# Mixture of experts: TensorE's order fixed by edges, weights asked for as far ahead as buffers allow, four single PSUM banks

## The chip, the core and the metric

The kernel is one program on one core of a Trainium2 chip. The metric is the device time of one execution in microseconds (us); lower is better. TensorE is called PE here, its loading of the stationary operand PEld, VectorE is DVE, ScalarE is ACT, GpSimd is POOL, and SP is the engine whose queue issues every load of weights.

## The reference

Two blocks of a small hybrid model run one after the other on 512 tokens of width 1024. The change lies in the last part of the first block, a mixture of experts:

```python
# 32 experts of width 512; each token has 2 experts with weights (gates)
def run(args):                       # a block of rows with one expert e
    tok_b, e = args
    xb = v_pad[tok_b]                # gather
    hu = xb @ w_e_in[e]              # (1024 x 1024)
    a, u = jnp.split(hu, 2, axis=-1)
    return (jax.nn.silu(a) * u) @ w_e_out[e]     # (512 x 1024)
ys = ys * rows_w[:, None]
out = jnp.zeros((T + 1, D)).at[rows_tok].add(ys) # scatter
```

All weights are float32. The experts hold 32 x (4 MB + 2 MB) = 192 MB of them, and each is read once.

## The kernel before

A list scheduler reorders the instructions that the code traces: it puts on each engine's queue what it holds to be ready first, so the order in the code is not the order on the engine. An engine then runs its queue strictly in that order.

**The experts stage** (`experts`) works on 16 pairs of experts, each expert with up to 64 rows. A pair's first product takes 8 slabs of `w_expert_in` for each of the two experts, its second product 4 slabs of `w_expert_out` for each. A slab is 128 x 1024 float32, 512 KB; a pair takes 24 slabs. `side_by_side` (line 1126) issues, for one slab of each expert and one half `c` of the columns, one product for expert 0 in the left 64 columns of the array and one for expert 1 in the right 64. Each such product is two MATMUL records in the profile, so a pair has 64 records with `sx` (first product) and 32 with `hT` (second).

**Around the products.** Every second pair, `gather` (line 1098) builds the rows `sx` of the next four experts by one-hot products: 8 units of 8 matmuls, each unit into one PSUM bank (`s`), which ACT or DVE copies away (line 1099). In the other pairs, `scatter` (line 1111) adds the results `y` of two pairs to `h`: 8 units of 4 matmuls, each unit into one `s` bank, which DVE adds (line 1113). After a pair's first product, ACT applies silu (line 1189), DVE multiplies (line 1190), and four PE transposes (line 1148) give `hT`, which the second product needs. In the code, three units stand ahead of the transposes and five behind. The second product of a pair stands two slab rows into the first product of the next pair.

**Buffers.** Slabs go through a ring of 22 buffers (10 + 12), with 7 more at the start (`raw_tile`). SP issues one load per slab and waits for a buffer whose products are done. PSUM has `self.banks(3, 0, 2)`: three tiles `g` of two banks for the products, and two single banks `s` for units and transposes.

**Overflow.** After pair 8, a branch (`overflow`, lines 1223 and 1232) reads a count; the loop behind it is for experts with more than 64 rows, and it is not entered in the profiled execution. It takes four buffers of the ring.

Of the kernel before, what the change touches and what calls it, by code (L numbers as in the profile page):

```python
# [3 lines left out]

# [14 lines left out]
P = 128  # L19
D = 1024  # L20
KT = D // P
NM = 16
S = 512
NT = S // P
# [6 lines left out]
NE = 32  # L31
ROWS = 64
OVER = 8
CAP = ROWS
HL = 4
EARLY = 7
RAWS = 10
RAWS2 = 12
# [78 lines left out]
class Builder:  # L117
# [781 lines left out]
        pool = self.early if early else self.mr if m < RAWS else self.mr2  # L899
        return self.t(pool, (P, D), tag="raw")  # L900

    def raw_slab(self, src):
        raw = self.raw_tile()
        self.nc.sync.dma_start(raw, src)
        return raw

    def proj_residual(self, first):

# [174 lines left out]
    def gather(self, xp, G):  # L1083

        nc, C = self.nc, self.C
        og = xp.tile([P, NT, 256], F32R, tag="og", name=self.nm("og"), bufs=1)
        for i in range(NT):
            a, b = (self.keyg[:, G, n * NT + i : n * NT + i + 1] for n in range(2))
            o = og[:, i]
            nc.vector.tensor_scalar(o, C["iota"][:, :256], a, None, OP.is_equal)  # L1090
            nc.vector.scalar_tensor_tensor(o, C["iota"][:, :256], b, o.bitcast(F32), OP.is_equal, OP.add)
        sx = xp.tile([P, KT, 256], F32, tag="sx", name=self.nm("sx"), bufs=1)
        yield sx
        for k in range(KT):
            p = self.p1()[:, :256]
            for hl in range(2):
                for i in range(NT):
                    nc.tensor.matmul(p, self.v[hl][:, i, k * P : (k + 1) * P], og[:, i], start=hl == 0 and i == 0, stop=hl == 1 and i == NT - 1)
            (nc.vector.tensor_copy if k % 2 else nc.scalar.copy)(sx[:, k], p)
            yield  # L1100

    def scatter(self, ys, last=False):

        nc, h2 = self.nc, self.h2
        more = [x[:, c] for x in (self.pg(), self.pg()) for c in range(2)] if last else []
        for n in range(2 * NT):
            i, c = n % NT, n // NT
            p = more.pop(0) if last and 2 <= n < 6 else self.p1()
            for a, (os_, y) in enumerate(ys):
                for hl in range(2):  # L1110
                    nc.tensor.matmul(p, os_[:, i * P : (i + 1) * P], y[c][:, hl], start=a == 0 and hl == 0, stop=a == len(ys) - 1 and hl == 1)
            x = h2[:, i, c * 512 : (c + 1) * 512]
            nc.vector.tensor_tensor(x, x, p, OP.add)
            yield

    def experts(self, es, early, routing):


        nc, io, C = self.nc, self.io, self.C
        xp = self.pool("ex", 2, es, side="right")  # L1120
        self.nraw = 0

        def side_by_side(out, x, ws, c, k, n):
            for e in range(2):
                o = slice(64 * e, 64 * e + 64)
                nc.tensor.matmul(out[o], x[:, o], ws[e][:, c * 512 : (c + 1) * 512], start=k == 0, stop=k == n - 1)  # L1126

        def slabs(src, pr, k):
            return [self.raw_slab(io[src][2 * pr + e][k * P : (k + 1) * P]) for e in range(2)]

        def one_hot(pr):

            os_ = yp.tile([P, S], F32R, tag="os", name=self.nm("os"), bufs=3)
            sid = C["slotid"][:, pr : pr + 1]
            kr, gr = self.rows
            t = yp.tile([P, S], F32, tag="ost", name=self.nm("ost"), bufs=1)
            nc.gpsimd.tensor_scalar(os_, kr[:, 0], sid, None, OP.is_equal)
            nc.gpsimd.tensor_scalar(t, kr[:, 1], sid, None, OP.is_equal)
            nc.gpsimd.tensor_tensor(os_, os_.bitcast(F32), t, OP.add)
            gs = self.t(yp, (P, 1), tag="gs")  # L1140
            junk = yp.tile([P, 2, S], BF, tag="junk", name=self.nm("junk"), bufs=1)
            nc.vector.scalar_tensor_tensor(junk, kr, sid, gr, OP.is_equal, OP.mult, accum_out=gs)
            return os_, gs

        def hidden_features(hu):
            pt = self.p1()
            for k in range(4):
                nc.tensor.transpose(pt[:, k * P : (k + 1) * P], hu[:, k * P : (k + 1) * P], C["ident"])
            hT = self.t(yp, (P, 4, P), tag="hT")
            nc.scalar.copy(hT, pt[:, :].rearrange("p (k s) -> p k s", k=4))  # L1150
            return hT

        def gated(py, gs):
            t = yp.tile([P, 2, 512], F32R, tag="y", name=self.nm("y"), bufs=4)
            nc.scalar.mul(t[:, 0], py, gs)
            nc.vector.scalar_tensor_tensor(t[:, 1], py, gs, t[:, 0].bitcast(F32), OP.mult, OP.subtract)
            return t

        def second(pr, hT, os_, gs):

            py = self.pg()
            for k in range(4):
                ws = slabs("w_expert_out", pr, k)
                for c in range(2):
                    side_by_side(py[:, c], hT[:, k], ws, c, k, 4)
            return os_, [gated(py[:, c], gs) for c in range(2)]

        self.banks(3, 0, 2)
        nxt = self.gather(xp, 0)
        sx = next(nxt)  # L1170
        self.run(nxt)
        done, pend = [], None
        for pr in range(NE // 2):
            last = pr == NE // 2 - 1
            ph = self.pg()
            for k in range(KT):
                if k == 2 and pend:
                    done.append(second(*pend))
                ws = slabs("w_expert_in", pr, k)
                for c in range(2):  # L1180
                    side_by_side(ph[:, c], sx[:, k, pr % 2 * P : pr % 2 * P + P], ws, c, k, KT)
            if pr == 0:
                early.close()
                yp = self.pool("exy", 2, es)
                for tag, w, bufs in (("y", 1024, 4), ("os", S, 3), ("hT", S, 2), ("gs", 1, 2), ("ost", S, 1), ("junk", S, 1)):
                    yp.tile([P, w], F32, tag=tag, name=self.nm(tag), bufs=bufs)
                self.run(routing)
            hu = self.t(xp, (P, 512), tag="hu")
            nc.scalar.activation(hu, ph[:, 0], AF.Silu)
            nc.vector.tensor_tensor(hu, hu, ph[:, 1], OP.mult)  # L1190
            if last:
                units = self.scatter(done)
                done = []
            elif pr % 2:
                units = self.gather(xp, pr // 2 + 1)
                sx = next(units)
            else:
                units = self.scatter(done) if pr else iter(())
                done = []
            for _ in range(3):  # L1200
                next(units, None)
            hT = hidden_features(hu)
            pend = (pr, hT) + one_hot(pr)
            self.run(units)
            if pr == OVER:
                self.overflow()

        pr, hT, os_, gs = pend
        ws = [slabs("w_expert_out", pr, k) for k in range(4)]
        y = []  # L1210
        for c in range(2):
            py = self.pg()[:, 0]
            for k in range(4):
                side_by_side(py, hT[:, k], ws[k], c, k, 4)
            y.append(gated(py, gs))
        self.run(self.scatter([(os_, y)], True))
        self.banks(2, 0, 4)

    def overflow(self):
# [1158 lines left out]
```

## Time and profile before

| | |
|---|---|
| median of 3 runs | 2713.28 us (2712.35 to 2714.08) |
| profiled execution, its own time | 2711.72 us |
| its span, first to last instruction | 2709.9 us |
| mean granted TensorE clock | 0.981 |
| PE busy | 2597.6 us (96% of the span) |
| DMA | 391.43 MB, mean 144 GB/s |

The time around the span is 1.8 us. A matmul's end in the profile is modelled and overlaps the next one, so PE's busy share says little; how far apart the starts of its rows lie says more. One row of a timeline merges instructions of one kind that follow each other.

### The profile page before, as it was taken

What the parts mean: (1) busy time and instruction counts of PE and PEld (TensorE: products, weight loads), DVE (VectorE), ACT (ScalarE), POOL (GpSimd) and SP (SyncE); (2) the same over time, 40 slices, a digit from 0 to 9 for tenths busy, and PEclk for the clock granted to TensorE, in tenths of its full rate; (3) what the DMA queues carried; (4) which work ended last, traced back from release to release, by engine and by line L of the source; (5) the groups of instructions that cost most, each with busy time, mean ns of one, the idle gap of its engine ahead of it and who ended that gap; (6) DMA issues with size and microseconds to landing.
All of it is one profiled execution on the core that took longest, in us unless ns stands there. A gap on an engine that the chain in (4) does not pass through costs nothing.

```text
span 2709.9 us, 40767 instructions
## 1 busy us (share of the span) xinstructions
PE 2597.6 (96%) x17262; PEld 2024.6 (75%) x17262; DVE 1125.4 (42%) x1744; ACT 880.9 (33%) x1496; POOL 350.9 (13%) x340
## 2 busy tenths in 40 slices
PE   7999999999899989998999998999999999899998
PEld 7887776777444444436999997898898778788887
DVE  4455455753322222225323336345455344632334
ACT  4345546623110000005222234336222253522222
POOL 0102112201211111102000013002233101200001
PEclk9999999999899999998999999999899999999999
DMA  4222223566699989983222223133111152132321
GB/s 127 79 63 76 74 60 89 154 206 231 260 419 367 379 312 403 377 309 101 84 89 93 95 94 101 42 91 87 44 52 41 48 148 71 63 109 82 105 94 63
DMA packets 294283, 391.43 MB, mean 144 GB/s; under 512 B 17472, under 2 KB 233024, under 8 KB 293840
## 3 DMA queue, kind: packets, MB, share of 16 engines
q1 hardware_dynamic: 294096, 388.78, 41.9%
q8 instruction: 137, 2.24, 0.3%
q14 instruction: 50, 0.41, 0.0%
HBM read 376.11 MB, written 12.62 MB: 143 GB/s over the span
## 4 chain that ended last, share of the span: by engine, by line
PE 47%; DVE 4%; ACT 2%; issue 1%; POOL 1%; POOLq 0%; DVEq 0%; ACTq 0%
PE g L277 37%; PE s L277 3%; PE s L2140 3%; DVE y L1551 1%; PE g L1825 1%; DVE y L1572 1%; DVE hres L1552 0%; DVE wlo L255 0%; ACT whi L253 0%; ACT dss L226 0%; PE s L2267 0%; PE s L1538 0%; PE s L1811 0%; PE g L1349 0%; ACT L226 0%
## 5 line engine op out<-in xcount | busy, mean ns | idle before, releaser
L255 DVE TENSOR_TENSOR wlo<-raw,whi 128x1024 fp32r<-128x1024 f32 (+1 forms) x277 | 333.7, 1215 | 401.0 <-ACT whi L253 398.8
L253 ACT CAST whi<-raw 128x1024 fp32r<-128x1024 f32 (+1 forms) x285 | 291.6, 1036 | 551.8 <-PE g L277 470.8
L277 PE MATMUL g<-x2h,whi 128*128 128x264 f32 (+1 forms) x1392 | 376.2, 326 | 1.7 <-ACT sz L2096 1.7
L277 PE MATMUL g<-x2l,whi 128*128 128x264 f32 (+1 forms) x1392 | 367.8, 321 | 0.0
L277 PE MATMUL g<-x2h,wlo 128*128 128x264 f32 (+1 forms) x1392 | 367.2, 320 | 0.0
L1126 PE MATMUL g<-raw,sx 128*64 128x512 f32 x1024 | 249.9, 598 | 0.0
L277 PEld LDWEIGHTS g<-x2h,whi 128*128 128x128 f32 x1392 | 230.8, 189 | 23.7 <-ACT sz L2096 2.1
L277 PEld LDWEIGHTS g<-x2h,wlo 128*128 128x128 f32 x1392 | 231.6, 189 | 19.2 <-issue 0.2
L277 PEld LDWEIGHTS g<-x2l,whi 128*128 128x128 f32 x1392 | 231.8, 189 | 17.9 <-issue 0.2
L277 PE MATMUL g<-uh,whi 128*128 128x264 f32 (+1 forms) x672 | 201.5, 344 | 7.1 <-ACT uh L283 4.6
L277 PE MATMUL g<-ul,whi 128*128 128x264 f32 (+1 forms) x672 | 199.3, 340 | 0.6 <-DVE ul L284 0.6
L277 PE MATMUL g<-uh,wlo 128*128 128x264 f32 (+1 forms) x672 | 199.5, 340 | 0.0
L1126 PEld LDWEIGHTS g<-raw,sx 128*64 128x64 f32 x1024 | 76.1, 137 | 139.8 <-issue 130.9
L1524 POOL TENSOR_TENSOR s<-s,q 128x256 f32<-128x256 f32 (+1 forms) x36 | 32.2, 908 | 860.0 <-ACT q L1522 858.7
L277 PEld LDWEIGHTS g<-uh,whi 128*128 128x128 f32 x672 | 117.9, 193 | 31.6 <-issue 8.8
L1126 PE MATMUL g<-raw,hT 128*64 128x512 f32 x512 | 135.5, 597 | 0.0
L277 PEld LDWEIGHTS g<-uh,wlo 128*128 128x128 f32 x672 | 118.1, 194 | 14.3 <-issue 2.4
L277 PEld LDWEIGHTS g<-ul,whi 128*128 128x128 f32 x672 | 117.5, 193 | 12.5 <-DVE ul L284 1.1
L277 PE MATMUL g<-x3h,whi 128*128 128x512 f32 x320 | 126.6, 396 | 0.0
L277 PE MATMUL g<-x3l,whi 128*128 128x512 f32 x320 | 126.6, 396 | 0.0
L277 PE MATMUL g<-x3h,wlo 128*128 128x512 f32 x320 | 126.6, 396 | 0.0
L1595 DVE TENSOR_TENSOR sa<-sa,g 128x528 f32<-128x528 f32 (+1 forms) x40 | 27.8, 696 | 200.1 <-PE g L277 200.1
(585 smaller groups left out, 4491.4 us busy)
## 6 DMA issues: line engine op xcount, KB each, us to landing
raw<-in_w_expert_in_dram SPq DMA_DIRECT2D x256, 512.0 KB, 7.9
raw<-in_w_expert_out_dram SPq DMA_DIRECT2D x128, 512.0 KB, 7.8
raw<-in_w_in_dram SPq DMA_DIRECT2D x112, 512.0 KB, 3.9
raw<-in_ffn_wi_dram SPq DMA_DIRECT2D x44, 1024.0 KB, 5.1
raw<-in_ffn_wo_dram SPq DMA_DIRECT2D x16, 1024.0 KB, 5.2
gates<-gx SPq DMA_DIRECT2D x24, 256.0 KB, 2.4
raw<-in_ffn_wo_dram SPq DMA_DIRECT2D x8, 768.0 KB, 4.7
raw<-in_w_hgrn_out_dram SPq DMA_DIRECT2D x8, 512.0 KB, 4.6
```

What stands on the lines that cost most here:

```text
L253: self.parts[0].append(nc.scalar.copy(hi[:, a:b], raw[:, a:b]))
L255: self.parts[1].append(lo_engine.tensor_tensor(lo[:, a:b], raw[:, a:b], hi[:, a:b].bitcast(F32), OP.subtract))
L277: nc.tensor.matmul(o, ww[:, k, c0 : c0 + m], xx[:, k, a:b], start=(k == 0 and n == 0), stop=(k == kt - 1 and n == 2),)
L1126: nc.tensor.matmul(out[o], x[:, o], ws[e][:, c * 512 : (c + 1) * 512], start=k == 0, stop=k == n - 1)
L1524: nc.gpsimd.tensor_tensor(self.sumsq[j], self.sumsq[j], sq, OP.add)
L1551: nc.vector.scalar_tensor_tensor(y, ys[:, k, a:b], gout[:, k : k + 1], r, OP.mult, OP.mult)
L1572: nc.vector.scalar_tensor_tensor(y, h[:, k, a:b], gin[:, k : k + 1], r, OP.mult, OP.mult)
L1595: nc.vector.tensor_tensor(view(sa), view(sa), su, OP.mult)
L1825: nc.tensor.matmul(p[:, r, :HT], l[:n, r, i], w[:n, r, i], start=i == 0 and l is ah and w is fh, stop=i == 4 and w is fl)
L2140: mm = lambda o, l, r: nc.tensor.matmul(o, l, r, start=True, stop=True)
```

## The change

`load_ahead` issues every load for which a ring buffer is free in the code's own account, ahead of the products that use it (with four buffers kept for the overflow). Each `with self.in_order()` block gives PE's instructions in it an edge to the last PE instruction traced before, so that they can't be put ahead of it. The three units, the transposes and the five units thereby stand behind a pair's products. `banks(2, 0, 4)` takes one `g` tile away and makes four `s` banks; the last scatter uses them alone.

```diff
+    def raw_free(self, n):
+        all_ = RAWS + RAWS2
+        if n >= all_ + EARLY:
+            n -= all_ if n >= all_ + EARLY + 9 else all_ + EARLY
+            return n not in self.held
+        return True
+    def load_ahead(self, spare=0):
+        while self.wants and self.raw_free(self.nraw + spare):
+            n, raw = self.nraw, self.raw_tile()
+            self.nc.sync.dma_start(raw, self.wants.popleft())
+            self.held[n] = raw
+    def next_raw(self):
+        ns = list(self.held)[:2]
+        def end(spare=0):
+            for n in ns:
+                del self.held[n]
+            self.load_ahead(spare)
+        return [self.held[n] for n in ns], end
+    def in_order(self):
+        return self.tc.issue_after(self.pe.ins) if self.pe else ExitStack()
...
-    def scatter(self, ys, last=False):
+    def scatter(self, ys):
...
-        more = [x[:, c] for x in (self.pg(), self.pg()) for c in range(2)] if last else []
...
-            p = more.pop(0) if last and 2 <= n < 6 else self.p1()
+            p = self.p1()
...
-        self.banks(3, 0, 2)
+        self.banks(2, 0, 4)
...
-            for k in range(KT):
-                if k == 2 and pend:
+            def first(a, b):
+                for k in range(a, b):
+                    ws, end = self.next_raw()
+                    for c in range(2):
+                        side_by_side(ph[:, c], sx[:, k, pr % 2 * P : pr % 2 * P + P], ws, c, k, KT)
+                    end(4 if pr == OVER else 0)
+            with self.in_order():
+                first(0, 2)
+            if pend:
+                with self.in_order():
                     done.append(second(*pend))
-                ws = slabs("w_expert_in", pr, k)
-                for c in range(2):
-                    side_by_side(ph[:, c], sx[:, k, pr % 2 * P : pr % 2 * P + P], ws, c, k, KT)
+            with self.in_order():
+                first(2, KT - 2)
+            if last or pr % 2 == 0:
+                units = self.scatter(done) if pr else iter(())
+                done = []
+            else:
+                units = self.gather(xp, pr // 2 + 1)
+                sxn = next(units)
+            with self.in_order():
+                first(KT - 2, KT)
...
-            for _ in range(3):
-                next(units, None)
-            hT = hidden_features(hu)
+            with self.in_order():
+                for _ in range(3):
+                    next(units, None)
+            with self.in_order():
+                hT = hidden_features(hu)
             pend = (pr, hT) + one_hot(pr)
-            self.run(units)
+            with self.in_order():
+                self.run(units)
```

**PE in pair 4's stretch, the second product of pair 3.** These are PE's rows of the kernel before; `hT` rows are second products (the two `raw` numbers in turn are the two experts), `y,os` rows are scatter units.

```order
L1126 MATMUL g_6937<-raw_6954,hT_6860 64x512
L1111 MATMUL s_7027<-y_6758,os_6670 128x512
L1126 MATMUL g_6937<-raw_6956,hT_6860 64x512
L1126 MATMUL g_6937<-raw_6954,hT_6860 64x512
L1126 MATMUL g_6937<-raw_6956,hT_6860 64x512
L1111 MATMUL s_7027<-y_6758,os_6670 128x512
L1111 MATMUL s_7033<-y_6758,os_6670 128x512 x2
L1126 MATMUL g_6937<-raw_6962,hT_6860 64x512
```

The same place of the changed kernel:

```order
L1163 MATMUL g_6981<-raw_6790,hT_6904 64x512
L1163 MATMUL g_6981<-raw_6792,hT_6904 64x512
L1163 MATMUL g_6981<-raw_6790,hT_6904 64x512
L1163 MATMUL g_6981<-raw_6792,hT_6904 64x512
L1163 MATMUL g_6981<-raw_6798,hT_6904 64x512
L1163 MATMUL g_6981<-raw_6800,hT_6904 64x512
```

Scatter matmuls stood between the products of the two experts; now the products of the two experts follow each other without a break.

**PE at the end of pair 4's first product.** Before, with the transposes (`hu`) right behind the last products and a product of the next pair:

```order
L1126 MATMUL g_6920<-raw_7018,sx_6824 64x512
L1126 MATMUL g_7090<-raw_7091,sx_6824 64x512
L1148 MATMUL s_7045<-consts_7_87,hu_7024 128x128 x4
L1111 MATMUL s_7060<-y_6758,os_6670 128x512 x2
L1111 MATMUL s_7060<-y_6970,os_6862 128x512 x2
```

And in the changed kernel:

```order
L1163 MATMUL g_6964<-raw_6971,sx_6849 64x512
L1136 MATMUL s_7071<-y_6802,os_6714 128x512 x2
L1136 MATMUL s_7071<-y_7014,os_6906 128x512 x2
L1136 MATMUL s_7077<-y_6802,os_6714 128x512 x2
L1136 MATMUL s_7077<-y_7014,os_6906 128x512 x2
L1136 MATMUL s_7083<-y_6802,os_6714 128x512 x2
L1136 MATMUL s_7083<-y_7014,os_6906 128x512 x2
L1182 MATMUL s_7089<-consts_7_87,hu_7068 128x128 x4
L1136 MATMUL s_7104<-y_6802,os_6714 128x512 x2
```

All eight scatter units now stand behind the last product, three of them ahead of the transposes.

**SP around the overflow.** Before, the queue reads the count (`TENSOR_LOAD`) and passes the branch among the loads:

```order
L904 DMA raw_7782<-in_w_expert_in_dram 128x1024
L1223 TENSOR_LOAD maxcount_6306
L1223 ISA x2
L904 DMA raw_8094<-in_w_expert_in_dram 128x1024
L904 DMA raw_8101<-in_w_expert_out_dram 128x1024
L904 DMA raw_8103<-in_w_expert_out_dram 128x1024
```

In the changed kernel:

```order
L915 DMA raw_7814<-in_w_expert_in_dram 128x1024
L915 DMA raw_7820<-in_w_expert_in_dram 128x1024
L915 DMA raw_7822<-in_w_expert_in_dram 128x1024
L1272 TENSOR_LOAD maxcount_6350
L1281 COMPARE_AND_BRANCH
```

Twelve more loads stand ahead of the branch than before. Elsewhere SP's loads stand in the order that they had. ACT's rows are in the same order throughout.

## Rows read from the trace of the kernel before

**Rows 1.** The page, bytes moved in 40 equal slices of 67.7 us.

```profile
GB/s 127 79 63 76 74 60 89 154 206 231 260 419 367 379 312 403 377 309 101 84 89 93 95 94 101 42 91 87 44 52 41 48 148 71 63 109 82 105 94 63
```

**Rows 2.** Windows of the stage: length, busy us of each engine, clock, DMA share, GB/s.

```profile
619.80:690.71 70.91, 55.18 (x272) 46.05 (x271) 33.19 (x65) 19.30 (x26) 17.17 (x10) 0.85 0.67 260
690.71:741.54 50.83, 50.71 (x265) 25.57 (x265) 13.30 (x34) 7.67 (x13) 15.08 (x10) 0.95 0.61 234
741.54:806.00 64.46, 63.88 (x314) 29.81 (x313) 17.13 (x31) 7.09 (x13) 8.73 (x6) 1.00 1.03 419
...
873.05:940.04 66.99, 64.73 (x297) 27.93 (x297) 16.53 (x30) 6.49 (x13) 8.73 (x6) 1.00 0.97 379
940.04:1013.60 73.56, 65.77 (x296) 31.71 (x296) 16.52 (x30) 6.50 (x13) 8.73 (x6) 0.95 0.85 320
1013.60:1080.68 67.08, 64.81 (x297) 27.98 (x297) 16.52 (x30) 6.50 (x13) 8.73 (x6) 1.00 1.01 403
...
1213.98:1234.05 20.07, 16.50 (x62) 6.79 (x62) 10.41 (x17) 6.81 (x10) 1.79 (x1) 1.00 0.52 161
```

**Rows 3.** Timeline of PE, pair 1 to pair 2: start, length, instructions.

```profile
741.54 0.73 PE L1098 MATMUL s<-og,vh 128*128 128x256 f32 x4
...
744.45 0.60 PE L1148 MATMUL s<-consts,hu 128*128 128x128 f32 x4
745.08 0.74 PE L1098 MATMUL s<-og,vh 128*128 128x256 f32 x4
...
749.95 3.65 PE L1126 MATMUL g<-raw,sx 128*64 128x512 f32 x16
...
770.70 2.11 PE L1111 MATMUL s<-y,os 128*128 128x512 f32 x8
```

**Rows 4.** Timeline of PE, the scatter after pair 2.

```profile
774.77 0.60 PE L1148 MATMUL s<-consts,hu 128*128 128x128 f32 x4
775.30 1.08 PE L1126 MATMUL g<-raw,sx 128*64 128x512 f32 x4
776.31 5.14 PE L1111 MATMUL s<-y,os 128*128 128x512 f32 x20
781.38 1.08 PE L1126 MATMUL g<-raw,sx 128*64 128x512 f32 x4
```

**Rows 5.** Timeline of PE inside pair 6; the bracket is idle time and its end.

```profile
883.07 4.45 PE L1126 MATMUL g<-raw,hT 128*64 128x512 f32 x18
887.46 0.50 PE L1111 MATMUL s<-y,os 128*128 128x512 f32 x1
887.89 1.93 PE L1126 MATMUL g<-raw,hT 128*64 128x512 f32 x6
889.75 0.96 PE L1111 MATMUL s<-y,os 128*128 128x512 f32 x3
...
899.26 8.80 PE L1126 MATMUL g<-raw,sx 128*64 128x512 f32 x40
909.47 0.66 PE L1148 MATMUL s<-consts,hu 128*128 128x128 f32 x4 [1.40 <-DVE hu L1190]
```

**Rows 6.** Timeline of PE behind pair 0: the rest of routing.

```profile
715.00 2.05 PE L1070 MATMUL s<-consts,key 128*128 128x128 f32 x16
716.98 1.07 PE L1126 MATMUL g<-raw,sx 128*64 128x512 f32 x2
717.99 2.05 PE L1070 MATMUL s<-consts,gates 128*128 128x128 f32 x16
719.87 0.25 PE L1077 MATMUL s<-M,onebf 128*128 128x32 bf16 x4
```

**Rows 7.** Waits of PE, 741.54 to 1213.98: us in total, times, longest.

```profile
PE s L1148 <- DVE hu L1190: 8.4, 6, 1.4
PE s L1098 <- PEq L1232: 5.6, 1, 5.6
```

**Rows 8.** Timeline of ACT at the stage's end.

```profile
1226.61 0.69 ACT L1155 ACTIVATE y<-g,gs 128x512 fp32r<-128x512 f32 x1 [9.97 <-PE g L1126]
```

More of the change, by code (lines that the diff above doesn't have):

```diff
@@ L2 @@
 from contextlib import ExitStack
+from collections import deque
 from itertools import chain
@@ L900, in raw_tile @@
         return self.t(pool, (P, D), tag="raw")
[L902 to L905, printed above, removed]
+    def raw_free(self, n):
[18 more added lines that the diff above has]
+        return self.tc.issue_after(self.pe.ins) if self.pe else ExitStack()
     def proj_residual(self, first):
@@ L1097, in gather @@
                 for i in range(NT):
-                    nc.tensor.matmul(p, self.v[hl][:, i, k * P : (k + 1) * P], og[:, i], start=hl == 0 and i == 0, stop=hl == 1 and i == NT - 1)
+                    self.pe = nc.tensor.matmul(p, self.v[hl][:, i, k * P : (k + 1) * P], og[:, i], start=hl == 0 and i == 0, stop=hl == 1 and i == NT - 1)
             (nc.vector.tensor_copy if k % 2 else nc.scalar.copy)(sx[:, k], p)
             yield
-    def scatter(self, ys, last=False):
+    def scatter(self, ys):
         nc, h2 = self.nc, self.h2
-        more = [x[:, c] for x in (self.pg(), self.pg()) for c in range(2)] if last else []
         for n in range(2 * NT):
             i, c = n % NT, n // NT
-            p = more.pop(0) if last and 2 <= n < 6 else self.p1()
+            p = self.p1()
             for a, (os_, y) in enumerate(ys):
                 for hl in range(2):
-                    nc.tensor.matmul(p, os_[:, i * P : (i + 1) * P], y[c][:, hl], start=a == 0 and hl == 0, stop=a == len(ys) - 1 and hl == 1)
+                    self.pe = nc.tensor.matmul(p, os_[:, i * P : (i + 1) * P], y[c][:, hl], start=a == 0 and hl == 0, stop=a == len(ys) - 1 and hl == 1)
             x = h2[:, i, c * 512 : (c + 1) * 512]
@@ L1120, in experts, with want @@
         xp = self.pool("ex", 2, es, side="right")
-        self.nraw = 0
+        self.nraw, self.held, self.wants, self.pe = 0, {}, deque(), None
+        def want(src, pr, n):
+            for k in range(n[0], n[1]):
+                self.wants.extend(io[src][2 * pr + e][k * P : (k + 1) * P] for e in range(2))
+        for pr in range(NE // 2):
+            want("w_expert_in", pr, (0, 2))
+            if pr:
+                want("w_expert_out", pr - 1, (0, 4))
+            want("w_expert_in", pr, (2, KT))
+        want("w_expert_out", NE // 2 - 1, (0, 4))
+        self.load_ahead()
         def side_by_side(out, x, ws, c, k, n):
@@ L1125, in side_by_side @@
                 o = slice(64 * e, 64 * e + 64)
-                nc.tensor.matmul(out[o], x[:, o], ws[e][:, c * 512 : (c + 1) * 512], start=k == 0, stop=k == n - 1)
-        def slabs(src, pr, k):
-            return [self.raw_slab(io[src][2 * pr + e][k * P : (k + 1) * P]) for e in range(2)]
+                self.pe = nc.tensor.matmul(out[o], x[:, o], ws[e][:, c * 512 : (c + 1) * 512], start=k == 0, stop=k == n - 1)
         def one_hot(pr):
@@ L1147, in hidden_features @@
             for k in range(4):
-                nc.tensor.transpose(pt[:, k * P : (k + 1) * P], hu[:, k * P : (k + 1) * P], C["ident"])
+                self.pe = nc.tensor.transpose(pt[:, k * P : (k + 1) * P], hu[:, k * P : (k + 1) * P], C["ident"])
             hT = self.t(yp, (P, 4, P), tag="hT")
@@ L1162, in second @@
             for k in range(4):
-                ws = slabs("w_expert_out", pr, k)
+                ws, end = self.next_raw()
                 for c in range(2):
                     side_by_side(py[:, c], hT[:, k], ws, c, k, 4)
+                end()
             return os_, [gated(py[:, c], gs) for c in range(2)]
-        self.banks(3, 0, 2)
+        self.banks(2, 0, 4)
         nxt = self.gather(xp, 0)
@@ L1175, in experts @@
             ph = self.pg()
-            for k in range(KT):
-                if k == 2 and pend:
-                    done.append(second(*pend))
-                ws = slabs("w_expert_in", pr, k)
-                for c in range(2):
-                    side_by_side(ph[:, c], sx[:, k, pr % 2 * P : pr % 2 * P + P], ws, c, k, KT)
+            def first(a, b):
+                for k in range(a, b):
+                    ws, end = self.next_raw()
+                    for c in range(2):
[5 more added lines that the diff above has]
+                with self.in_order():
+                    done.append(second(*pend))
+            with self.in_order():
[8 more added lines that the diff above has]
+                first(KT - 2, KT)
+            if pr % 2:
+                sx = sxn if not last else None
             if pr == 0:
@@ L1186, in experts @@
                     yp.tile([P, w], F32, tag=tag, name=self.nm(tag), bufs=bufs)
-                self.run(routing)
+                with self.in_order():
+                    self.run(routing)
             hu = self.t(xp, (P, 512), tag="hu")
@@ L1190, in experts @@
             nc.vector.tensor_tensor(hu, hu, ph[:, 1], OP.mult)
[L1191 to L1199, printed above, removed]
-            for _ in range(3):
-                next(units, None)
-            hT = hidden_features(hu)
+            with self.in_order():
[3 more added lines that the diff above has]
+                hT = hidden_features(hu)
             pend = (pr, hT) + one_hot(pr)
-            self.run(units)
+            with self.in_order():
+                self.run(units)
             if pr == OVER:
@@ L1208, in experts @@
         pr, hT, os_, gs = pend
-        ws = [slabs("w_expert_out", pr, k) for k in range(4)]
+        ws = list(self.held.values())
         y = []
@@ L1213, in experts @@
             for k in range(4):
-                side_by_side(py, hT[:, k], ws[k], c, k, 4)
+                side_by_side(py, hT[:, k], ws[2 * k : 2 * k + 2], c, k, 4)
             y.append(gated(py, gs))
-        self.run(self.scatter([(os_, y)], True))
+        self.run(self.scatter([(os_, y)]))
         self.banks(2, 0, 4)
```

## Prediction

> **What bounds the kernel now.** I read the page's slices first: the bytes moved are near 400 GB/s in slices 12 to 17 and far below elsewhere [rows 1]. That is the experts stage, and the change touches nothing outside it. Then windows cut at the starts of the gathers, which repeat every second pair [rows 2]: one period of two pairs takes 66.99 or 67.08 us, 73.56 where the overflow's branch stands, and the seven stretches from the gather after pair 1 (741.54) to the end of pair 15's first product (1213.98) sum to 472.4 us. DVE is busy for 16.5 us of a period, ACT for 6.5, POOL for 8.7; PE for 64.7 of 67.0. So only PE and the stream of weights can bound it.
>
> The stream: a period needs 48 slabs of 0.524 MB, 25.17 MB. In the best window it ran at 419 GB/s with the DMA engines' share at 1.03 [rows 2], which makes 60.1 us a period, 1.25 us a slab. In the other windows it ran at 379, 320 and 403. It is not the bound, though not far from it: it had 6.9 us to spare in each period.
>
> So PE. Does it do 67.0 us of work? The timeline has an undisturbed stretch [rows 3]: from 741.54 to 749.95 three gather units, the transposes, five units; from 749.95 to 770.70 the 96 records of pair 2's stretch. That is 8.41 + 20.75 = 29.16 us, 0.216 a record. The scatter after pair 2 has 20 matmuls in 5.07 us, 0.2535 each, and its transposes take 0.53 [rows 4]. The other half of a period, undisturbed, is then 32 x 0.2535 + 0.53 + 20.75 = 29.4 us. Together **58.55 us of work in a period of 67.0**.
>
> Where the 8.5 us go is seen inside pair 6 [rows 5]. A scatter matmul between the products of the two experts leaves one product without its partner in the other half of the array: 24 records and one scatter matmul take 6.68 us (883.07 to 889.75), against 24 x 0.216 + 0.25 = 5.4. So 1.2 us is lost there. The timeline of the period from 873.05 to 940.04 has eight such insertions (five of scatter, three of gather), and the transposes wait 1.40 for `hu` [rows 5]. (8.5 - 1.4) / 8 = 0.9 us an insertion, near the 1.2.
>
> A rule of the Trainium skill names another cause. "TensorEngine Tiling (Array Packing)", section "Key Properties", says that changing the tiling mode drains TensorE. Were a switch all that an insertion costs, its price would be in another row: four records, both halves paired, between matmuls of the full array take 1.01 us (775.30 to 776.31, [rows 4]) against 0.86, so 0.15. Eight insertions would be worth 1.2 us and, with the wait, a period 2.6, 18 us in all. The lost partner, which rows 5 show, is worth more than the switch, and the sum goes by rows 5.
>
> **The change part by part.**
>
> *The order of the products* is the main term. As the order's rows show, the products of the two experts now follow each other unbroken, and units stand in a lump behind them. All seven periods become what rows 3 and 4 show: 58.55 us. The four `s` banks can only help a lump: with two, scatter matmuls are paced by DVE's add. Bound from below: a gather matmul of 256 columns takes 4.87 / 40 = 0.122 us (745.08 to 749.95, [rows 3]), twice that is 0.243 for 512 columns, 7.8 us instead of 8.1, period 58.2. I take 58.4.
>
> *Three units ahead of the transposes* cover ACT's silu and DVE's product: PE stood 1.4 us idle for them [rows 5], and three units last 2.91 us (741.54 to 744.45, with no wait behind them [rows 3]) or 12 x 0.25 = 3.0. In total PE waited 8.4 us for `hu` in the seven stretches [rows 7]; this is inside the 8.5 a period and not counted twice. If the cover were gone it would cost 14 x 1.4 = 20 us.
>
> *Two `g` tiles instead of three* cost nothing: a tile is wanted again a whole product later, and its readers on ACT and DVE take a few us within products of 20.75.
>
> *The loads.* SP's order is unchanged but around the overflow, so I give the longer look ahead no term of its own. A faster PE makes the stream the next candidate: 60.1 us a period against 58.4, 12 us in seven. What hides it is the lead. By 741.54 the stream had moved 260 x 70.91 + 234 x 50.83 = 30.3 MB [rows 2], 57 slabs and, less some small loads, about 55; PE had used 40. Fifteen slabs are 18.8 us, more than the 12. The stop of PE at the overflow gives back some 6 more. So PE still binds, narrowly.
>
> *The overflow* costs PE 73.56 - 66.99 = 6.6 us now [rows 2], 5.6 of them idle [rows 7]. The idle part stays, as the branch does. Twelve more loads stand ahead of it on SP, so the stream should no longer starve there (320 GB/s in that window). Its bounds are 5.6 and, if the four buffers taken from the ring hold up four slabs, 6.6 + 5. I take 6.6. The stretch from 741.54 to 1213.98 becomes 7 x 58.4 + 6.6 = 415.4 instead of 472.4: **minus 57.0**.
>
> *The start.* From 715.00 to 741.54 are 26.5 us. In order, they are the products for keys and gates (1.98 + 1.88), 0.2 for the counts, 0.6 for transposes and 20.75 for pair 1's stretch [rows 6, 3]: 25.4. Four banks let the keys and gates run through. **Minus 1.1.**
>
> *The end.* From pair 15's first product to the last add of `h` are 20.07 us [rows 2]: 12.63 to ACT's first `y` [rows 8] and 7.44 after it. The scatter of pair 14, which now stands whole behind the product, had six matmuls done earlier (1.5 us), and in the last second product the two halves of the columns are interleaved with some same-half neighbours, up to 4 x 0.43. Some of that is saved on insertions there. **Plus 1.1**, between 0 and 3.
>
> Sum: -57.0 - 1.1 + 1.1 = -57. The profiled execution took 2711.7 us (2709.9 and 1.8 around it), so **2655 us**. The median of the runs is 2713.3, 1.6 above that execution; I leave this in the range.
>
> **The rivals.**
>
> *The weights become the bound.* For it: 1.25 us a slab is all that the best window shows, and 58.4 a period would need 431 GB/s. Against it: the lead above. With no use of the lead a period is 60.1, 7 x 60.1 + 6.6 = 427.3, a gain of 45: 2667. At the 403 GB/s of another window, where the share was also 1.01, a period is 62.5 and, with the overflow hidden in the stream, 437 in all, 35 gained: 2677.
>
> *The lump stalls PE*: `hu` late, or banks not freed in time, 1.4 to 2 us in each of 14 pairs, 20 to 28 us given back: 2675 to 2683. Against it: rows 3 run this very lump with two banks.
>
> *Only the switches are saved*, 18 us as worked out above: 2693. The lost partner in rows 5 speaks against it.
>
> *Nothing changes*, since the stream already sets the 67.0 (a mean of 375 GB/s): 2712. Against it: 419 GB/s over 64 us, and PE's starts without a gap for weights. Beside this stands a rule that speaks against the change: "DMA: Bandwidth & Descriptors" of the Trainium skill, section "Where 436 GB/s comes from", has loads from HBM bound at about 358 GB/s a core. By it a period could not fall below 25.17 / 0.358 = 70.3 us (an estimate from that page). The trace does not agree: it has periods of 67.0 and windows of 419 and 403 GB/s.
>
> *Slower*: while PE runs a lump, no buffer comes free, and if SP is then held and the stream stops, a pair costs 24 x 1.25 = 30.0 us for its slabs plus the lump, 8.4: 38.4, 76.8 a period, 9.8 x 7 = 69 us more: 2780. It decides from a stop of 3.5 us a pair (half of 67.0 - 60.1). Against it: the window with the lump at 741.54 has 419 GB/s; 22 buffers hold 27 us of stream.
>
> **How the numbers follow.** Forecast (2646 to 2664 by the bounds above) 0.63; weights bind (2660 to 2677) 0.24; lump stalls 0.05; only the switches 0.02; no change 0.03; slower 0.03. The range 2646 to 2671 holds the first and most of the second. A measurement of this kernel can tell about 0.2%, 5.4 us. Faster by more than that: 0.63 + 0.24 + 0.05 + 0.02 = 0.94; within it 0.03; slower 0.03.
>
> **What would show it.** Right: gathers 58 to 59 us apart; 96 records in 20.7 us in every stretch; no idle time of PE ahead of the transposes; the branch's 5.6 us still there; GB/s of 415 to 425 in most windows. The stream as the bound would show as PE's weight loads waiting for `raw` and gathers 60 us or more apart; stalled lumps as PE waiting for `hu`, DVE or ACT. The prediction is wrong if a period stays above 62 us, or if the products, though unbroken in order, start one by one as slabs land.

## The result, and the profile of the changed kernel

| | before | changed |
|---|---|---|
| median | 2713.47 us | 2652.09 us (2650.69 to 2653.9, 4 runs) |
| ratio | | 0.9775, 95% interval 0.9758 to 0.9792 |
| profiled execution; its span | 2711.72; 2709.9 us | 2650.69; 2648.9 us |

The change makes the kernel 61 us faster. The forecast was 2655, in a range of 2646 to 2671. The profiled execution, which the forecast was added up for, took 2650.69. The total hides that two of its terms were wrong in opposite directions, so the parts are read one by one.

The page of the changed kernel, bytes moved in 40 slices (of 66.2 us each), answers to [rows 1]:

```profile
GB/s 130 81 65 77 76 53 79 139 224 178 261 419 419 419 387 419 419 283 81 96 88 88 96 83 85 72 88 77 46 49 41 57 143 68 85 89 90 99 96 64
```

In slices 12 to 17 the weights now come at 419 without a break, but for one slice with 387. Windows cut at the starts of the gathers, as in [rows 2] (length, busy us of PE, PEld, DVE, ACT and POOL, clock, DMA share, GB/s); the first is the start, the last begins where pair 15's first product ends:

```profile
689.86:738.07 48.21, 48.21 (x265) 24.58 (x265) 13.30 (x34) 7.67 (x13) 15.44 (x10) 0.96 0.63 244
738.07:795.63 57.56, 57.56 (x298) 27.91 (x296) 16.70 (x30) 6.61 (x12) 8.74 (x6) 1.00 1.03 419
795.63:853.20 57.57, 57.57 (x299) 27.92 (x297) 16.70 (x30) 6.62 (x12) 8.74 (x6) 1.00 1.03 419
853.20:910.76 57.56, 57.56 (x298) 27.91 (x296) 16.70 (x30) 6.62 (x12) 8.74 (x6) 1.00 1.03 419
910.76:974.18 63.42, 59.33 (x298) 29.81 (x296) 16.70 (x30) 6.62 (x12) 8.72 (x6) 0.97 0.95 386
974.18:1033.36 59.18, 59.01 (x298) 28.60 (x296) 16.70 (x30) 6.61 (x12) 8.74 (x6) 1.00 1.03 419
1033.36:1093.62 60.26, 60.07 (x297) 28.98 (x297) 16.70 (x30) 6.61 (x12) 8.73 (x6) 1.00 1.03 419
1093.62:1153.46 59.84, 59.67 (x298) 28.87 (x297) 13.92 (x21) 6.92 (x13) 2.84 (x2) 1.00 1.03 419
1153.46:1180.40 26.94, 16.25 (x69) 8.42 (x68) 18.85 (x26) 10.22 (x16) 6.21 (x3) 0.89 0.70 252
```

Three things are to be seen. The first three periods take 57.57 us, below the 58.4 that was forecast. The last three take 59.2 to 60.3, though PE has the same work. And the period with the branch takes 63.42, 5.85 above its neighbours before it. From 738.07 to 1153.46 are 415.39 us, where the forecast had 415.4.

The timeline of PE in pair 4 shows the order that the change fixes; before, units stood inside the products [rows 5]. The first and the last row are cut off by the ends of the view:

```profile
814.53 10.04 PE L1163 MATMUL g<-raw,sx 128*64 128x512 f32 x46
824.50 3.02 PE L1136 MATMUL s<-y,os 128*128 128x512 f32 x12
827.36 0.60 PE L1182 MATMUL s<-consts,hu 128*128 128x128 f32 x4
827.71 4.80 PE L1136 MATMUL s<-y,os 128*128 128x512 f32 x20
832.45 3.65 PE L1163 MATMUL g<-raw,sx 128*64 128x512 f32 x16
835.93 2.31 PE L1163 MATMUL g<-raw,hT 128*64 128x512 f32 x10
```

Read by the starts, the scatter's matmuls take 0.237 us each (4.74 / 20) and the transposes 0.35, where [rows 4] had 0.2535 and 0.53. All waits of PE from 738.07 to 1153.46 (us in total, times, longest), against [rows 7]:

```profile
PE g L1163 <- PEq L1281: 4.1, 1, 4.1
PE g L1163 <- DMA raw<-in_w_expert_in_dram: 0.5, 3, 0.2
```

The wait for `hu` is gone. PE's own waits do not show the 6.6 us by which the late periods are longer. They show one row further up, where PE loads its stationary operand, and in what SP waits for. In the first three periods the same row of PEld has 3.1, and no period is longer for it, so the row alone proves nothing; an experiment below does. The rows that follow are those of PEld from 974 to 1154, and of SP from 738 to 1153 (its row for the branch, L1281, is read further down):

```profile
PEld g L1163 <- DMA raw<-in_w_expert_in_dram: 6.9, 12, 1.0
```

```profile
SPq L915 <- DMA raw<-in_w_expert_in_dram: 171.4, 202, 1.7
SPq L915 <- DMA raw<-in_w_expert_out_dram: 90.4, 104, 2.1
SPq L915 <- PE g L1163: 21.0, 42, 4.1
SPq L1281 <- SPq L1281: 9.7, 1, 9.7
```

SP used to wait for PE's products; now it waits for its own transfers. In the kernel before, from 741 to 1214, its largest row was this:

```profile
SPq L904 <- PE g L1126: 235.8, 191, 7.6
```

### The profile page after: what moved, and what is told of

The parts are those of the page before. It is cut to its first block, busy times and chain, and to the rows that moved or that the text cites. A ratio compares the mean times of both kernels' runs of the same rounds, so it can differ in the third digit from the quotient of the medians.

```text
span 2648.9 us, 40785 instructions
## 1 busy us (share of the span) xinstructions
PE 2553.3 (96%) x17262; PEld 2025.6 (76%) x17262; DVE 1126.3 (43%) x1744; ACT 881.9 (33%) x1496; POOL 351.5 (13%) x340
## 4 chain that ended last, share of the span: by engine, by line
PE 54%; DVE 4%; ACT 2%; DMA 2%; issue 1%; POOL 1%; POOLq 0%; DVEq 0%; SPq 0%; ACTq 0%
PE g L278 38%; PE g L1163 4%; PE s L278 4%; PE s L2189 3%; DMA raw<-in_w_expert_in_dram 2%; PE s L1124 1%; PE s L1136 1%; DVE y L1600 1%; PE g L1874 1%; DVE y L1621 0%; DVE hres L1601 0%; DVE wlo L256 0%; DMA raw<-in_w_expert_out_dram 0%; ACT whi L254 0%; ACT dss L227 0%
## 5 line engine op out<-in xcount | busy, mean ns | idle before, releaser
L1163 PE MATMUL g<-raw,sx 128*64 128x512 f32 x1024 | 233.6, 598 | 4.6 <-PEq L1281 4.1
L1163 PE MATMUL g<-raw,hT 128*64 128x512 f32 x512 | 112.7, 592 | 0.0
```

Of the source, the lines that this page charges most:

```text
L1163: self.pe = nc.tensor.matmul(out[o], x[:, o], ws[e][:, c * 512 : (c + 1) * 512], start=k == 0, stop=k == n - 1)
```

## The experiments

In all of them "the stage" means the time from the start of the second gather to the start of the last product with `sx`, in the profiled execution. It is 471.8 us in the kernel before and 414.9 in the changed one. The program around the stage, nearly the same in all of them, varies from one execution to the next by some 2 us ahead of it and 3 us behind it, so the stage tells more than the total. An insertion is a group of full-array matmuls that stands between two products of a pair; a run is what stands between two such groups; a lone product is the one left without a partner where a run has an odd number of products; a lump is a row of units behind a pair's first product.

**What does a unit among the products cost?** Two kernels put five of each scatter's eight units one by one among the first products. They differ from each other only in where the units stand. The cut shows the lines that differ, shortened; in both, the scatter is also set up ahead of the products, and every product has its edge.

```diff
 for e in range(2):                       # runs of even length
+    if e == 0: next(mid)                 # c == 1, rows 3 to 7
     matmul(out[o], ...)

 for e in range(2):                       # runs of odd length
+    if e == k % 2 and c == k % 2: next(mid)
     matmul(out[o], ...)
```

> The changed kernel, but in each of the eight scatters five of the eight units stand one by one among the first products, each behind a whole pair of products (expert 0 and expert 1), so that 40 insertions are added and no product loses its partner. Theory of the prediction (an insertion costs because a product is left without a partner): only the switch is paid, 0.15 us each, five a period, so the first three periods go from 57.57 to about 58.3 and the kernel to 2651 to 2657 us. Rival (any insertion costs 0.9 to 1.2 us, whatever stands beside it): a period of 62.6, and 35 to 40 us less some 7 that PE now waits for the stream, 2678 to 2685 us.

> The same five units of each scatter as in the run with even runs, but placed so that each run of products between two of them has an odd number: six products a scatter are left alone, 48 in all. Theory of the prediction: beside the switches (0.15 each) a lone product takes 0.43 us more, as it is not halved by its neighbour in the other half of the array: a period of 57.57 + 0.75 + 2.6 = 60.9 where PE is the bound, the kernel 12 to 20 us above the run with even runs, 2667 to 2675 us. Rival (only the switch costs, or every insertion the same): no difference from the run with even runs.

Measured: even runs 2660.91 us, ratio 0.9806 (0.9791 to 0.9821); odd runs 2678.69, ratio 0.9872 (0.9857 to 0.9887). An undisturbed period of each, even runs first:

```profile
797.86:857.27 59.41, 59.41 (x298) 27.19 (x297) 16.62 (x30) 6.62 (x12) 8.74 (x6) 1.00 1.03 419
```

```profile
801.27:863.23 61.96, 61.96 (x299) 27.99 (x297) 16.71 (x30) 6.62 (x12) 8.73 (x6) 1.00 1.02 409
```

Against 57.57 an insertion with even runs costs (59.41 - 57.57) / 5 = 0.37 us; six lone products cost a further 2.55, 0.42 each. The timelines show both. With even runs:

```profile
819.01 1.20 PE L1136 MATMUL s<-y,os 128*128 128x512 f32 x4
820.14 1.94 PE L1167 MATMUL g<-raw,sx 128*64 128x512 f32 x8
822.00 1.20 PE L1136 MATMUL s<-y,os 128*128 128x512 f32 x4
```

With odd runs, where a single product (two records) stands between two units:

```profile
830.10 1.20 PE L1136 MATMUL s<-y,os 128*128 128x512 f32 x4
831.23 1.07 PE L1167 MATMUL g<-raw,sx 128*64 128x512 f32 x2
832.23 1.18 PE L1136 MATMUL s<-y,os 128*128 128x512 f32 x4
```

By the starts, eight paired records take 1.86 us, against 8 x 0.216 = 1.73, and four scatter matmuls 1.13 against 0.95: a switch in and a switch out, 0.13 and 0.18, together 0.31 of the 0.37. Two records alone take 1.00, where half of a pair takes 0.43. So the lost partner is real, and the switch is dearer than the 0.15 of the forecast, which counted one side of it. The even runs missed their 2651 to 2657 by 4 us, partly for this reason and partly because their period with the branch takes 67.54, 8.1 above its neighbours instead of 5.85. The odd runs came 17.8 above the even ones, inside the 12 to 20 expected, and so 3.7 above the 2667 to 2675 that stood on the other forecast.

**Which part makes the gain?** Four kernels take one part alone or leave one out. The cuts show the line that matters; with the banks alone, the last scatter uses the single banks as in the changed kernel, and the loads at use have a few lines more.

```diff
-        self.banks(3, 0, 2)          # the kernel before, banks alone
+        self.banks(2, 0, 4)

-        return self.tc.issue_after(self.pe.ins) if self.pe else ExitStack()
+        return ExitStack()           # the changed kernel, no edges

-        self.banks(2, 0, 4)          # the changed kernel, two banks
+        self.banks(3, 0, 2)

-        self.load_ahead()            # the changed kernel, loads at use
...
     def next_raw(self):
+        self.load_ahead(2)           # only until two slabs are held
```

> The kernel before with four single banks and two tiles for the products, and nothing else of the change. Its order on PE has 73 insertions into the products and 68 products without a partner (before: 70 and 54). Theory (order and partners make the gain): 14 lone products more at the 0.42 us that the runs with even and odd runs gave, plus 6 us, less up to 0.7 a period for a faster lump, 5: 2708 to 2720 us. Rival (the evictions of two banks pace PE, the banks make the gain): 2652 to 2670 us.

> The changed kernel without the edges; look-ahead and four banks stay. The scheduler then has 68 insertions into the products and 60 lone products instead of 16 and 2. Theory: 52 x 0.37 + 58 x 0.42 = 43.6 us of PE's time, of which the 7 to 10 that PE waits for the stream in the changed kernel are taken off: 2684 to 2690 us, and more where the transposes lose their cover. Rival (look-ahead and banks make the gain): 2650 to 2660 us.

> The changed kernel with two single banks and three tiles for the products, as before. Theory of the prediction (banks are a small term): scatter matmuls go from 0.237 back to 0.2535 us, 0.5 a period, and the transposes from 0.35 to 0.53; where the stream is the bound this is hidden: 2650 to 2656 us. Rival (the lump is paced by evictions and needs four banks): 2660 us or more.

> The changed kernel with each load traced at its use, as before, no look-ahead. SP's order is then the same but around the branch, where 11 loads move from ahead of it to behind it. Theory (the look-ahead itself is worth nothing, as SP's order hardly changes): the stream keeps 419 GB/s, only the period with the branch differs: 2650 to 2657 us. Rival (the look-ahead is what gives the stream its rate): periods above 62 and 2670 us or more.

| kernel | median, us | ratio (95%) | stage, us |
|---|---|---|---|
| before with four banks | 2711.41 | 0.9993 (0.9983 to 1.0002) | 474.2 |
| changed, no edges | 2699.28 | 0.9949 (0.9934 to 0.9964) | 462.7 |
| changed, two banks | 2660.33 | 0.9809 (0.9796 to 0.9823) | 420.5 |
| changed, loads at use | 2654.13 | 0.9780 (0.9767 to 0.9793) | 416.9 |
| changed, once more | 2652.36 | 0.9781 (0.9768 to 0.9795) | 415.8 |

The last line is the changed kernel measured once more, which came as expected:

> The changed kernel once more, for comparison in the same call: 2650 to 2654 us; seven periods as in its first profile (three of 57.6, one of 63.4, two of 59 to 60.3).

The edges make the gain: without them the stage is 47.8 us longer. The time is 9 us above the top of what was expected for the order alone; PE's waits, from 739 to 1203, tell of the rest:

```profile
PE g L1163 <- ACT sx L1125: 4.9, 5, 1.0
PE s L1182 <- DVE hu L1245: 3.8, 5, 1.4
PE g L1163 <- PEq L1281: 1.6, 1, 1.6
PE s L1136 <- DVE y L1190: 1.4, 6, 0.3
```

43.6 for insertions and lone products and 10.1 for the waits for `sx`, `hu` and `y` are 53.7. Of this go 6.6, which PE loses to the stream in the changed kernel, and 2.5, as its stop at the branch is 1.6 instead of 4.1: 44.6. Some 3 of the 47.8 us stay open. The banks alone change nothing in the total. With them the scheduler leaves 73 insertions and 68 lone products instead of 70 and 54; by the prices above that is 7 us more, and faster lumps give some time back. That the two cancel is argued from these counts. Under the edges the banks are worth more than "a small term": with two of them (and three tiles for the products) an undisturbed period takes 59.06, 1.5 more. Here is its scatter:

```profile
826.12 3.31 PE L1136 MATMUL s<-y,os 128*128 128x512 f32 x12
829.27 0.60 PE L1182 MATMUL s<-consts,hu 128*128 128x128 f32 x4
830.21 5.14 PE L1136 MATMUL s<-y,os 128*128 128x512 f32 x20 [0.34 <-DVE h L1138]
```

Beside pair 4 above, the twelve matmuls take 3.15 instead of 2.86, the transposes with the wait behind them 0.94 instead of 0.35, the twenty 5.07 instead of 4.74. In the stage this is 7 x 1.5 = 10.5 us of PE's work and 1.6 more in the period with the branch (66.50, 7.4 above its neighbours), less the 6.6 of stream that PE's longer work now hides: 5.5 of the 5.6 measured. The 2650 to 2656 that this run was expected to give fell; the rival's bound of 2660 was just met, with runs from 2656.3 to 2665.4, though the scale of the rival's cause (evictions set the lump's pace) is 8 us, not the gain. The look-ahead is worth nothing that can be told.

**Are the late periods bound by the stream?** One kernel loads fewer slabs from pair 5 on (the last products of expert 1 read the slabs of expert 0, so a part of the weights is left out while PE's work stays), one has the branch late, one has no branch.

```diff
-  self.wants.extend(io[src][2 * pr + e][...] for e in range(2))
+  one = src == "w_expert_in" and pr >= 5 and k >= KT - 2
+  self.wants.extend(io[src][2 * pr + e][...] for e in range(1 if one else 2))

-OVER = 8
+OVER = 14                            # late; 15 in the last run of this section

-            if pr == OVER:           # no branch
-                self.overflow()
```

> The changed kernel with two of 24 slabs of each pair not loaded from pair 5 on: the products of expert 1 with the last two slab rows of the first weight read the slabs of expert 0 instead (this part of the weights is left out; PE's instructions stay). Theory (from about pair 10 on the stream of weights is the bound, since the lead of 15 slabs is used up and the overflow stops the stream for 5 us): the last three periods fall from 59.2 to 60.3 to the 57.6 of the first three, together 6.6 us less, 2644 us; the period with the overflow stays near 63.4. Rival (the late periods are longer because of PE, its clock or the units): they stay, 2650 us.

> The changed kernel with the overflow's branch after pair 14 instead of pair 8. Theory (the branch stops the stream for 5 us, which the late periods pay): with no stop until the last loads are on their way, seven periods of about 57.6 and once 5.9 for the branch, 409 instead of 415.4, so 2643 to 2646 us. Rival 1 (the late periods are stream-bound whatever the branch does, since 60.1 a period is all that the stream gives): 2649 to 2652. Rival 2 (at the end nothing covers the branch, and the four buffers that it takes hold up the last loads): 2655 or more.

> The changed kernel without the overflow (its branch, its buffers and its loop are left out; no expert overflows in this run, so the output is the same). Theory: SP stands at the branch from 949.95 to 959.68 until its loads in flight have landed, and the stream loses 4.9 us; without it the stream is continuous and is the bound from the fifth period on, at 59.9 to 60.1 a period: 415.4 - 4.9 = 410.5 from the second gather to the end of pair 15's first product, 2645 to 2647 us. Rival 1 (only PE's own stop of 5.85 us counts and PE is the bound): periods of 57.57 throughout, 403, 2638 us. Rival 2 (nothing, since the late periods take up the difference): 2650 us.

Fewer bytes: 2643.3 us, ratio 0.974 (0.9725 to 0.9755), stage 409.2. Its period with the branch and the two behind it:

```profile
912.34:976.64 64.30, 60.27 (x299) 29.19 (x297) 16.71 (x30) 6.61 (x12) 8.72 (x6) 0.95 0.91 357
976.64:1034.20 57.56, 57.56 (x298) 27.91 (x297) 16.71 (x30) 6.61 (x12) 8.74 (x6) 1.00 1.03 419
1034.20:1091.77 57.57, 57.57 (x299) 27.93 (x297) 16.71 (x30) 6.61 (x12) 8.74 (x6) 1.00 1.02 409
```

With 2 of 24 slabs less the late periods fall to the 57.57 of the early ones. The stream was their bound. Branch late: 2653.5, ratio 0.9784 (0.9771 to 0.9798), stage 416.2: no gain, 1.5 us above what the first rival allowed and as much below the second. Both have a part in it, as its last three periods show:

```profile
969.04:1028.97 59.93, 59.75 (x298) 28.89 (x297) 16.70 (x30) 6.61 (x12) 8.73 (x6) 1.00 1.03 419
1028.97:1088.87 59.90, 59.70 (x297) 28.88 (x296) 16.71 (x30) 6.61 (x12) 8.73 (x6) 1.00 1.03 419
1088.87:1154.88 66.01, 61.89 (x297) 29.72 (x296) 13.07 (x21) 6.91 (x13) 2.82 (x2) 0.95 0.94 381
```

Without a stop the stream still becomes the bound, and at the end the branch costs 6.1 us. Without the branch: 2648.29, ratio 0.9754 (0.9741 to 0.9768), stage 411.5, 3 to 4 us less, where 4.9 was expected, and 1.3 above the expected 2645 to 2647. Its periods where the branch was and behind it:

```profile
912.76:971.07 58.31, 58.31 (x298) 28.32 (x296) 16.71 (x30) 6.62 (x12) 8.73 (x6) 1.00 1.03 419
971.07:1031.68 60.61, 60.31 (x298) 29.03 (x297) 16.71 (x30) 6.61 (x12) 8.73 (x6) 1.00 1.03 419
1031.68:1091.59 59.91, 59.71 (x297) 28.91 (x296) 16.71 (x30) 6.61 (x12) 8.73 (x6) 1.00 1.03 419
```

So even an unbroken stream overtakes PE in the fourth period; rival 1, 403 us for the stage, fell. What the branch does to the stream is in two views of the changed kernel: windows around it (the columns as above), and SP's 9.7 us at L1281 in its waits.

```profile
948.00:956.00 8.00, 4.26 (x14) 1.63 (x16) 0.38 (x1) 0.00 (x0) 7.72 (x6) 0.80 1.02 411
956.00:964.00 8.00, 8.00 (x40) 3.27 (x38) 0.00 (x0) 0.00 (x0) 0.29 (x1) 0.99 0.46 161
964.00:972.00 8.00, 8.00 (x40) 3.20 (x38) 2.79 (x4) 1.37 (x2) 0.00 (x0) 1.00 1.02 419
```

161 instead of 419 over 8 us is a loss of 4.9 us of stream. The trace has the last load ahead of the branch issued at 949.02 and landed at 959.67; SP goes on at 959.68, so it stands there until its own loads have landed. A branch behind the last load should then cost the stream nothing, so this was tried:

> The changed kernel with the overflow's branch after pair 15, where every load of the experts' weights stands ahead of it on SP. Theory: without the branch in its midst the stream is 3.3 us faster, as in the run without the branch, and PE's stop at the branch (4 to 5 us) lies for the most part beside the wait for the last slabs, which land some 5 us after the first product of pair 15 ends: 0 to 3 us less than the changed kernel in the same call. Rival (at the end nothing lies beside the stop, and the next stage's loads stand behind the branch on SP): 2 to 6 us more.

Measured: 2652.68, ratio 0.9785 (0.9771 to 0.9798). The stage has 412.5 us, like the kernel without the branch, but PE then stands at the branch:

```profile
1159.84 7.09 PE L1163 MATMUL g<-raw,hT 128*64 128x512 f32 x32 [3.36 <-SPq L1281]
```

What the stream gains, PE loses there: the time is 0.3 us above the changed kernel measured beside it, between the two expectations. The changed kernel as it is was not beaten by a kernel that keeps all weights and the overflow.

**The cover of three units.**

```diff
-                for _ in range(3):
+                for _ in range(0):
                     next(units, None)
```

> The changed kernel with no unit ahead of the transposes; all eight stand behind them. Theory of the prediction (three units cover the silu and the product): PE stands idle 1.4 to 2 us ahead of the transposes in 14 pairs, 20 to 28 us, of which 7 to 10 are hidden by the wait for the stream: 2661 to 2672 us. Rival (the wait is short, or lies wholly beside the stream): 2650 to 2655 us.

Measured: 2664.67, ratio 0.9823 (0.9808 to 0.9838), stage 423.4; periods of 60.5. PE's waits, 739 to 1163:

```profile
PE s L1182 <- DVE hu L1245: 20.2, 14, 1.4
```

Fourteen waits of 1.4 us, as the forecast had it; some 12 of the 20 are hidden, by the 6.6 of the stream and by the branch's period, which is only 2.3 above its neighbours.

## Why the prediction was right, and where it was not

**PE bounds, and its order costs it**: right for the kernel before. The insertions and lost partners cost what rows 5 said. With the runs' prices the 54 insertions that the change takes away are worth 54 x 0.37 = 20 us, and the 52 lone products 52 x 0.42 = 22; that is 0.78 an insertion, where 0.9 was taken. `hu` adds 8.4 and the banks, by the run with two of them, up to 7 x 1.5 = 10.5: 61 of the 63.6 by which PE's work fell (472.4 to 408.8, below). The rival "only the switches are saved" had too low a price for them and was still wrong: the odd runs cost 18 us more with the same number of switches. The Trainium skill, "TensorEngine Tiling (Array Packing)", section "Key Properties", says that a change of tiling mode drains TensorE. The traces agree that it costs something, 0.13 to 0.18 us each way, but the lost partner costs about as much again; that this cost is a drain is not shown by any run.

**A period of 58.4**: 57.57. The failed step is the bound "from below" for the banks. 58.55 was put together from rows with two banks, and four were given 0.15 of the 0.35 between the bounds. The run with two banks takes 59.06, 0.5 more than that, most of it the wait behind the transposes; and four banks are worth 1.5: besides the scatter's matmuls the transposes start without waiting for a bank, which the forecast had left at 0.53 and 0.60. The term was mis-sized by 7 x 0.83 = 5.8 us.

**PE still binds, narrowly**: this step failed. PE binds for three periods, then the stream does, for 1.6 + 2.7 + 2.3 = 6.6 us. The working gave the stream 60.1 us a period and a lead of 18.8 us, and 7 x (60.1 - 57.57) = 17.7 would have fitted. The kernel without the branch shows how much lead there was: three periods of 57.57 and one of 58.31 used 3 x 2.5 + 1.8 = 9.3 us, then it was gone. The lead was counted in bytes moved. But a slab takes 9.9 us from issue to landing, so at 1.25 us a slab about eight are on their way at once, and bytes of a slab that has not landed are of no use to PE. This is the page of the changed kernel, DMA issues:

```profile
raw<-in_w_expert_in_dram SPq DMA_DIRECT2D x256, 512.0 KB, 9.9
```

The loads that the kernel without the branch had issued by its second gather (560 to 740.07):

```profile
raw<-in_w_expert_in_dram SPq DMA_DIRECT2D x41, 512.0 KB, 7.9
raw<-in_w_expert_out_dram SPq DMA_DIRECT2D x16, 512.0 KB, 10.0
```

That is 57 slabs. Less eight on their way, 49 have landed, and PE had begun 40: the lead is nine slabs, 11.3 us (an estimate from these rows), where the forecast had 15 and 18.8. Of the 11.3, 9.3 were used before PE had to wait; the last 2 us stay open. The rival "the weights become the bound" described the last three periods, not the kernel.

**The two errors cancel**: 7 x 57.57 + 5.85 = 408.8 of PE's work, plus 6.6 of stream, are 415.4. The forecast of 7 x 58.4 + 6.6 was the same number for another reason, and that is luck. The 4 us by which the profiled execution is below 2655 come from the start (2.4) and the end (1.9). Of the signs named in the forecast, the 96 records in 20.7 us, the missing wait ahead of the transposes and the 419 GB/s came; gathers 58 to 59 us apart did not. The bounds of its terms add up to 2651 to 2663, so no term stood behind 2646.

**The overflow**: 5.85 against 6.6. PE stands 4.1 us idle and runs the next sixteen records in 5.15 us (951.74 to 956.89) instead of 3.48. The granted clock, 1.00 from 944 to 948 and from 964 on, falls to 0.50 there, the level of 1.2 GHz:

```profile
953.00:955.00 2.00, 2.00 (x6) 0.61 (x4) 0.00 (x0) 0.00 (x0) 1.82 (x3) 0.50 1.02 412
```

The bound of 5 us more, for buffers that hold up slabs, had the right size and the wrong cause: the stream does stop for 4.9 us, but for SP's wait at the branch. Moving the loads ahead of the branch did not prevent that.

**No term for the look-ahead, none for two `g` tiles, cover by three units**: the runs with loads at use and without cover bear the first and the third out; the second was not tried by itself.

**The start**: -3.5 against -1.1. From pair 0's end to the second gather it is 25.09 us (712.98 to 738.07) instead of 26.54, -1.45, near what was forecast. The rest was not forecast and can't be put down to the change: the first gather begins 0.85 us earlier and takes 9.23 instead of 10.41. Its first matmuls run at 0.21 us each, at a granted clock of 0.50 (1.2 GHz, 689.86 to 692.00), the later ones at 0.12, at 1.00 (2.4 GHz, 694 to 696), and when the one gives way to the other varies. In the kernels above with four banks and the same gather, in the same order, it took from 9.04 us (mean granted clock 0.84) to 10.29 (0.72); with two banks under the edges it took 9.85 (0.79). The mean is 0.81 in the changed kernel and 0.73 in the kernel before.

**The end**: from pair 15's first product to the last add of `h` 19.28 us instead of 20.07, -0.8 against +1.1. The forecast feared up to 4 x 0.43 for lone halves in the last second product; its 32 records take 7.14 us, where a second product inside the stage takes 7.04 (835.93). That part of the term was not there; the eight adds follow each other in one row of 4.87 us.

## What to carry to other kernels

When two products share the array as here, count how many run without a partner before counting switches: what stands between them is cheap only if it leaves runs of even length. When the order is mended, ask at once what the next bound is, and measure a prefetch's lead by the landing of whole tiles ahead of their use, not by the bytes moved. A total that comes as forecast is no evidence for its terms; one row for each term is.

## What the runs showed of the hardware

- A product of two records alone in the array takes 1.00 us between full-array matmuls; eight records in partners take 1.86.
- A single unit of four full matmuls among half-array products costs 0.37 us, 0.18 of it in its own matmuls, although the profile shows no wait of PE there.
- At a branch that is not taken SP stands 9.7 us, until the last load issued ahead of it has landed (959.67, SP goes on at 959.68), and the stream loses 4.9.
- After PE's stop of 4.1 us the granted clock was 0.50 (1.2 GHz) from 953 to 955, while PE ran products without a gap, and the sixteen records there took 1.7 us more.
